# Token groups of 256 and 272, a tail by token groups, down's first operands ahead of up's last pairs, and the residual's squares taken in down

## The chip, the cores and the metric

The kernel runs on one core of a Trainium2 chip. The metric is the device time of one execution in microseconds (us). The core has five engines with an instruction queue each: TensorE (PE in the profile, with PEld for its weight loads), VectorE (DVE), ScalarE (ACT), GpSimd (POOL) and SyncE (SP), which here does nothing but issue DMA transfers. An engine takes its instructions in the order of its queue. SBUF is the working memory, PSUM the memory that matmuls write to, DRAM the memory outside.

## The reference, cut to what matters

One layer of a streaming encoder over 1056 tokens (1024 of a new stream, 32 of a running one), with a model width of 1024 and a feed-forward width of 4096, all in float32:

```python
h = rms_norm(x, ln1_g)
proj = h @ w_in                       # q, k, v of 4 heads; a, b of a gated unit
u = proj_a * sigmoid(proj_b)
a = diff_attention(q, k_all, v_all)   # two softmaxes per head, their difference times v
c = conv(u); c = layer_norm(c); c = c * sigmoid(c)
x = x + concat([a, c]) @ w_out        # output projection
h2 = rms_norm(x, ln2_g)
x = x + square(relu(h2 @ w_up)) @ w_down
y = rms_norm(x, ln_f_g)               # y, and k, v and the last frames of u, are returned
```

## The kernel before

Activations lie transposed, with channels on the 128 partitions and tokens along the free dimension. Every matrix product is made of three: both operands are split into a high and a low part of a faster float type (`split`, `split_to`, `w_split`: a copy on ScalarE for the high part, a subtraction on VectorE or GpSimd for the low part), and high·high, high·low and low·high are summed in PSUM (`products`, L101, and `mm1`, L987). The work is written in program order; a framework gives each engine's queue its order by a simulation of the whole kernel, so instructions of one engine may stand in another order than written, and it gives tiles their slots: a pool has so many slots (`bufs`), and a new tile waits until a slot's earlier tile was read for the last time.

The stages are these.

*Start.* `x_load` loads token tiles of 128 (the ninth has 32), `x_stat` takes the sum of squares of each token (L262), `x_group` transposes a set of tiles (`XSET`: three, two, two, two tiles), copies it to SBUF (L282) and makes the normalized operand with its split (L291 to L296). `load_block` loads and splits a block of `w_in`.

*Dense.* `dense` multiplies a block of 128 output channels with one of four token groups (`GRP`: four times 264 columns; `GW` is 264 and `HT` 528, half of the tokens). Attention, convolution and their norms run between the blocks. The first two blocks run group by group, as `x_group` delivers.

*Output projection.* Parts of `w_out` are multiplied early (`out_part`, L832); the loop at L956 does the rest by token group and block `ob`, adds into the residual stream `x2` (L962) and calls `rows_in`, which squares the sum on ScalarE (L907), adds the squares up over the blocks on GpSimd into `ssacc` (L908), scales by the norm's weight and splits. `b_sums` (L919) makes sums of the operand's quarters on VectorE, `spill` stores `x2` to DRAM as `x2d`. The row's scale is not applied before up: it is squared by the activation and taken out in the final norm, so down's residual is scaled by it instead.

*Up and down.* Both products go by seven products of half blocks instead of eight. Up's operands are named by these products, 1 to 7 (`BX`), and lie in tiles of 128x4x528 ("quads") in three pools, `act[0]` and `act[1]` with four slots each and `q2` with eight. Up runs over sixteen pairs of 128 output channels. Each pair stores seven tiles of results to DRAM (`ud`); the last two pairs run step by step side by side. `row_stat` (L1107) sums `ssacc` over the partitions, and `row_scales` loads the result back in two forms: `vb`, on all partitions, and `rs2`, a column per final tile (L1189).

Down runs over four chunks (`c`) of seven products each, in the order 1, 2, 6, 7, 4, 5, 3 (`PRODS`). A product has four units `m` of 24 matmuls of 264 columns. Its operand is loaded from `ud` (`u_load`, L1220) and split (`u_split`); its weights are loaded from `w_down` (`d_a`), summed (L1232 to L1235) and split. `d_run` runs a product and adds it to its accumulators (L1244). At four products (`RES`) a quarter of the residual is loaded from `x2d`, scaled by `vb` (L1201) and added (L1204).

*Tail.* `final(j)` is the last norm of one token tile of `FT`: eight transposes (L1297), squares with their sum on ScalarE (L1302), a step on VectorE (L1303), the power −1/2 on GpSimd (L1304), two products on VectorE (L1305, L1306), and the store. In the last chunk `fin_step` puts these between the units: tiles 0 to 4 from product 5 on, 5 to 7 in the second half of product 3, 8 to 10 behind everything.

Of the kernel before, what the change touches and what calls it, by code (L numbers as in the profile page):

```python
# [51 lines left out]
def hybrid_step(ctx: ExitStack, tc: tile.TileContext, t):  # L52
# [72 lines left out]
    def act_groups(hi, lo):  # L125

        return [
            [[a[k // 4][g // 2][:, k % 4, GW * (g % 2) : GW * (g % 2) + GW] for k in range(KC)] for a in (hi, lo)]
            for g in range(4)
        ]  # L130
# [636 lines left out]
    x_load(2)  # L767
# [5 lines left out]
    for j in range(3):  # L773
        x_stat(j)
# [94 lines left out]
    sqp = ph2.enter_context(tc.tile_pool(name="sqp", bufs=2, reuse_waits="tile"))  # L869
    ssacc = bigp.tile([P, TOK], F32, tag="big", name="ssacc")  # L870
# [29 lines left out]
    def rows_in(ob, c0, n):  # L900

        xs = x2[ob][:, c0 : c0 + n]
        if ob == 0:
            nc.scalar.activation(ssacc[:, c0 : c0 + n], xs, AF.Square)
        else:
            sq = sqp.tile([P, GW], F32, tag="sq", name="sq2")[:, 0:n]
            nc.scalar.activation(sq, xs, AF.Square)  # L907
            nc.gpsimd.tensor_tensor(ssacc[:, c0 : c0 + n], ssacc[:, c0 : c0 + n], sq, ALU.add)  # L908
        kh, k, th, s = ob // 4, ob % 4, c0 // HT, slice(c0 % HT, c0 % HT + n)
        nc.scalar.activation(B[kh][th][:, k, s], xs, AF.Copy, scale=pcol[:, 12 + ob : 13 + ob])  # L910
        if th == 0:
            split_to(B[kh][0][:, k, s], Bs[kh][0][:, k, s], Bs[kh][1][:, k, s])
# [42 lines left out]
    for g in range(4):  # L955
        for ob in range(3, KC):  # L956
            ps = psM.tile([P, 512], F32, tag="mm", name="pw")
            v = ps[:, 0:GW]
            products(v, wo[ob], PARTS[2] if ob < 6 else [4, 5, 6, 7, 0, 1, 2, 3], slice(0, P), *cx[g])
            c0, w = GRP[g]  # L960
# [22 lines left out]
    def mm1(out, w, b, hb, first):  # L983

        seq = [(w[i], b[j], k) for i, j in ((0, 0), (0, 1), (1, 0)) for k in range(4)]
        for n, (wi, bj, k) in enumerate(seq):
            nc.tensor.matmul(  # L987
                out, wi[:, k, :], bj[:, k, GW * hb : GW * hb + GW],
                start=first and n == 0, stop=n == len(seq) - 1, skip_group_check=not first,
            )  # L990

    def mm(ps, w, b, first):

        for hb in range(2):
            mm1(ps[:, hb, 0:GW], w, b, hb, first)
# [63 lines left out]
    def up_steps(p, ws, ps1):  # L1059
# [25 lines left out]
        t3 = tTp.tile([P, HT], F32, tag="tT", name="o3")  # L1085
        sub(p1, pre, u11)
        sub(t3[:], c22, p1)
        store(p, 0, t0)
        dma(ud[6, p], t3[:])
# [5 lines left out]
        sub(pre, c21, t3[:])  # L1095
        store(p, 4, t2)

    rsd = dram.tile([1, TOK], F32, tag="rsd", name="rsd")

    def row_stat():  # L1100

        v = bigp.tile([P, 2, HT], F32, tag="big", name="vrow")
        for th in range(2):
            ps = acc_tile()
            for hb in range(2):
                c0 = HT * th + GW * hb
                nc.tensor.matmul(ps[0:1, hb, 0:GW], ones[:], ssacc[:, c0 : c0 + GW], start=True, stop=True)  # L1107
            nc.vector.tensor_scalar(halves(v[0:1, th, :]), ps[0:1, :, 0:GW], 1.0 / D, EPS, ALU.mult, ALU.add)
        dma(rsd[:], v[0:1].rearrange("p b n -> p (b n)"))
# [28 lines left out]
    up_load(1, act[0])  # L1138
    nxt = up_s(0, False)
    up_p2(*pend1)  # L1140
    row_stat()

    for p in range(NP_ - 2):
        ws = nxt
        ps1 = up_p1(p) if p >= NPRE else None
        up_load(p + 2, (q2, act[0])[p % 2])
        if p + 1 < NP_ - 2:
            nxt = up_s(p + 1, p + 1 >= NPRE)
        for _ in up_steps(p, ws, ps1):
            pass  # L1150
    last = [NP_ - 2, NP_ - 1]
    by = {}
# [28 lines left out]
    FT = [(P * j, P) for j in range(4)] + [(4 * P, HT - 4 * P)] + [(HT + 88 * j, 88) for j in range(6)]  # L1181
    rs2 = sm2.tile([P, 16], F32, tag="rs2", name="rs2", bufs=1)
    vb = lnp.tile([P, TOK], F32, tag="vb", name="vb")

# [30 lines left out]
    UVAR = {1: 0, 2: 4, 6: 6, 7: 2, 4: 5, 5: 1, 3: 3}  # L1215
    ops_u, raw_u = {}, {}

    def u_load(c, i):
        raw_u[c, i] = quad(act[0], "du")[:]
        dma(raw_u[c, i], ud[UVAR[i], 4 * c : 4 * c + 4].rearrange("k p n -> p k n"))  # L1220

    def u_split(c, i):
        ops_u[c, i] = split_to(raw_u.pop((c, i)), quad(q2, "dh", F32R)[:], quad(q2, "dl", F32R)[:])

# [28 lines left out]
    held = {}  # L1253

    def d_run(c, i, w):
        end = c == NCH - 1
        u = ops_u.pop((c, i))
        if end and i == 3:

            for hb in range(2):  # L1260
                for m in range(4):
                    if m % 2 == 0:
                        ps = acc_tile()
                    mm1(ps[:, m % 2, 0:GW], w[m], u, hb, True)
                    add(ACC[5][m][:, GW * hb : GW * hb + GW], ps[:, m % 2, 0:GW])
                    fin_step()
                if hb == 0:
                    fin.extend([lambda: None] + [lambda j=j: final(j) for j in range(5, 8)])
            return
        second = i in (2, 4, 3)  # L1270
        for m in range(4):
            ps = held.pop(m) if second else acc_tile()
            if i in (1, 7, 5) and not (end and i == 5):
# [8 lines left out]
            if end and i == 5:  # L1282
                add(halves(ACC[5][m]), v)
                fin_step()
# [3 lines left out]
        if end and i == 4:  # L1288
            fin.extend([lambda: None] + [lambda j=j: final(j) for j in range(5)])


    def final(j):
# [7 lines left out]
        ss = sm2.tile([P, 2], F32, tag="ssf", name="ssf")[:n, 0:1]  # L1300
# [14 lines left out]
    for c in range(NCH):  # L1315

        loads.extend([
            [("a", c, 0), ("u", c, 1)], [("a", c, 1), ("u", c, 2)], [("a", c, 2), ("a", c, 3), ("u", c, 6)],
# [8 lines left out]
    RES = {(1, 2): (0, 0), (1, 4): (1, 0), (2, 2): (0, 1), (2, 4): (1, 1)}  # L1327
    load_step()
    load_step()
    u_split(*seq[0])  # L1330
    nw = w_prep(*seq[0])
    for n, (c, i) in enumerate(seq):
# [5 lines left out]
        if (c, i) == (0, 3):  # L1338
            row_scales()
# [5 lines left out]
        d_run(c, i, w)  # L1345
        if (c, i) in RES:
# [3 lines left out]
    for j in range(8, 11):  # L1350
        final(j)
# [65 lines left out]
```

## Time and profile before

| | |
|---|---|
| time, median of 3 runs | 1224.98 us (1224.97 to 1226.77) |
| profiled execution: its own time | 1224.9 us |
| its span, from the first to the last instruction | 1223.1 us |
| mean granted clock of TensorE | 0.994 of full speed |
| TensorE busy | 1176.2 us, 96% of the span, 9340 matmuls |
| VectorE busy | 887.9 us, 73% |
| ScalarE busy | 580.9 us, 47% |
| GpSimd busy | 142.1 us, 12% |
| DMA | 157.15 MB, 128 GB/s in the mean |

The profile is of one execution on the chip. Busy time counts an engine's instructions, without its waits. Matmuls are pipelined and the profile's ends are modelled, so the duration of one (about 0.28 us) is longer than the distance from one start to the next. A releaser in the lists of waits is inferred from semaphores.

### The profile page before, as it was taken

To read this page: it belongs to the slowest core of one execution; us is meant where nothing else is said; L and a number is where in the kernel's file an instruction comes from. 1 tells how busy PE (TensorE), PEld (TensorE's weight loads), DVE (VectorE), ACT (ScalarE), POOL (GpSimd) and SP (SyncE) were. 2 spreads that over 40 slices of the span, in tenths; PEclk is the share of its full clock that TensorE was granted. 3 is DMA by queue.
4 is the path that set the end of the run, shared out by engine and by line. 5 is a ranking of instruction groups with operands and counts; after the bars stand their busy time and mean duration, and the time that the engine had idled before them with its cause. 6 is when DMAs were issued, how large, how long until landed. Compare 5 with 4: busy or idle time off the path is not lost. (4 is left out here: it accounts for less than half of the span.)

```text
span 1223.1 us, 23089 instructions
## 1 busy us (share of the span) xinstructions
PE 1176.2 (96%) x9340; PEld 1131.1 (92%) x9340; DVE 887.9 (73%) x1494; ACT 580.9 (47%) x1160; POOL 142.1 (12%) x149
## 2 busy tenths in 40 slices
PE   6999999999899999989999999999999999999995
PEld 5889988898888789989999999999999999999995
DVE  5797795799975644687776565665865978978865
ACT  7434345433488543665444444444745343333323
POOL 3111122022231221350000000000000000000001
PEclk9999999999999999999999999999999999999998
DMA  6531122122233422234554343445964354454003
GB/s 221 194 101 53 37 66 80 54 62 60 64 110 111 125 89 69 107 97 139 197 190 156 135 152 140 149 142 184 330 225 150 135 188 171 160 193 141 18 23 120
DMA packets 126410, 157.15 MB, mean 128 GB/s; under 512 B 7889, under 2 KB 79458, under 8 KB 126304
## 3 DMA queue, kind: packets, MB, share of 16 engines
q1 hardware_dynamic: 124640, 152.74, 37.3%
q0 software_dynamic: 1664, 2.95, 0.9%
q8 instruction: 73, 1.20, 0.4%
q14 instruction: 33, 0.27, 0.1%
HBM read 104.32 MB, written 51.35 MB: 127 GB/s over the span
## 5 line engine op out<-in xcount | busy, mean ns | idle before, releaser
L987 PE MATMUL pf<-dh,wlo 128*128 128x264 f32 x896 | 144.9, 284 | 2.8 <-DVE wlo L877 2.8
L987 PE MATMUL pf<-dl,whi 128*128 128x264 f32 x896 | 146.9, 286 | 0.0
L987 PE MATMUL pf<-dh,whi 128*128 128x264 f32 x896 | 146.3, 286 | 0.0
L876 ACT ACTIVATE whi<-da 128x512 fp32r<-128x512 f32 x96 | 60.3, 631 | 145.2 <-PE pf L987 141.0
L987 PEld LDWEIGHTS pf<-dh,wlo 128*128 128x128 f32 x896 | 124.1, 189 | 3.0 <-DVE wlo L877 3.0
L987 PEld LDWEIGHTS pf<-dl,whi 128*128 128x128 f32 x896 | 125.0, 189 | 0.0
L987 PEld LDWEIGHTS pf<-dh,whi 128*128 128x128 f32 x896 | 123.4, 189 | 0.1
L101 PE MATMUL pm<-hTh,whi 128*128 128x264 f32 x640 | 107.3, 294 | 6.9 <-ACT tT L347 2.3
L876 ACT ACTIVATE whi<-praw 128x512 fp32r<-128x512 f32 x86 | 53.6, 628 | 107.8 <-PE pf L987 61.6
L78 POOL TENSOR_TENSOR wlo<-raw,whi 128x512 fp32r<-128x512 f32 (+1 forms) x55 | 77.4, 1422 | 229.0 <-PE pm L101 161.0
L101 PE MATMUL pm<-hTh,wlo 128*128 128x264 f32 x640 | 103.8, 287 | 0.0
L101 PE MATMUL pm<-hTl,whi 128*128 128x264 f32 x640 | 102.2, 286 | 1.0 <-DVE hTl L296 1.0
L101 PEld LDWEIGHTS pm<-hTh,whi 128*128 128x128 f32 x640 | 87.2, 188 | 14.0 <-issue 3.2
L101 PEld LDWEIGHTS pm<-hTl,whi 128*128 128x128 f32 x640 | 87.3, 188 | 2.1 <-DVE hTl L296 1.4
L101 PEld LDWEIGHTS pm<-hTh,wlo 128*128 128x128 f32 x640 | 87.8, 188 | 1.3 <-issue 1.3
L1067 DVE TENSOR_TENSOR o<-pf,o 128x528 f32<-128x528 f32 x80 | 56.1, 703 | 44.9 <-PE pf L987 44.7
L1304 POOL TENSOR_TENSOR ssf<-ssf,mhalf 88x1 f32<-88x1 f32 (+2 forms) x11 | 6.0, 547 | 669.4 <-DVE ssf L1303 669.4
L877 DVE TENSOR_TENSOR wlo<-praw,whi 128x512 fp32r<-128x512 f32 x86 | 58.6, 685 | 27.4 <-ACT whi L876 13.4
L877 DVE TENSOR_TENSOR dl<-du,dh 128x2112 fp32r<-128x2112 f32 x28 | 65.9, 2354 | 9.8 <-ACT dh L876 9.4
L1244 DVE TENSOR_TENSOR xa<-pf,xa 128x528 f32<-128x528 f32 (+1 forms) x72 | 48.0, 671 | 34.0 <-PE pf L987 33.9
L877 DVE TENSOR_TENSOR wlo<-da,whi 128x512 fp32r<-128x512 f32 x96 | 64.9, 681 | 10.5 <-ACT whi L876 5.5
L531 ACT ACTIVATE p<-ps,mn 128x128 f32<-128x128 f32 (+6 forms) x64 | 47.4, 742 | 35.2 <-DVE mn L524 30.8
(300 smaller groups left out, 2732.8 us busy)
## 6 DMA issues: line engine op xcount, KB each, us to landing
du<-ud SPq DMA_DIRECT2D x28, 1056.0 KB, 6.0
ud<-o SPq DMA_DIRECT2D x48, 528.0 KB, 3.9
praw<-in_w_up SPq DMA_DIRECT2D x16, 1024.0 KB, 5.5
da<-in_w_down SPq DMA_DIRECT2D x16, 1024.0 KB, 7.5
raw<-in_w_in SPq DMA_DIRECT2D x40, 256.0 KB, 3.0
xTd<-xT SPq DMA_DIRECT2D x8, 528.0 KB, 2.7
x<-xTd SPq DMA_DIRECT2D x8, 528.0 KB
x2d<-x SPq DMA_DIRECT2D x16, 264.0 KB, 2.0
```

The lines of the kernel that those rows point to most:

```text
L78: (eng or nc.vector).tensor_tensor(lo[:], raw, hi[:].bitcast(F32), ALU.subtract)
L101: nc.tensor.matmul(out, w[k][a][:, cols], b[k], start=i == 0, stop=i == len(seq) - 1)
L531: nc.scalar.activation(p[:, 0:nk], sc[m], AF.Exp, bias=mn[:, 2 + m : 3 + m], scale=-1.0, accum_out=s0 if m == 0 else s1[:, 0:1],)
L876: nc.scalar.activation(hi, raw, AF.Copy)
L877: nc.vector.tensor_tensor(lo, raw, hi.bitcast(F32), ALU.subtract)
L987: nc.tensor.matmul(out, wi[:, k, :], bj[:, k, GW * hb : GW * hb + GW], start=first and n == 0, stop=n == len(seq) - 1, skip_group_check=no ...
L1067: add = lambda o, ps, b: nc.vector.tensor_tensor(halves(o), ps, halves(b), ALU.add)
L1244: nc.vector.tensor_tensor(o, ps, o, ALU.add)
L1304: nc.gpsimd.tensor_tensor(ss, ss, mhalf[:n, 0:1], ALU.pow)
```

## The change

- `GRP` becomes (0, 256), (256, 272), (528, 272), (800, 256), and `XSET` two, three, two, two tiles. The third token tile is loaded with the second set. The sums of squares of tiles 0 and 1 are taken on VectorE.
- The squares and their sums in `rows_in` are left out. In down, at the products in `SQR`, a quarter of `x2d` is loaded, squared on ScalarE and summed on VectorE into `vb`; `row_stat` and `row_scales` come after product 6 of the second chunk, and the residual steps at later products.
- Two quads of up lie in other pools. Ahead of the last two pairs, down's operands (0, 1) and (0, 2) are loaded into `q2`, and the first is split there. The last pairs' tile `o3` lies in `q2` too.
- The last chunk's products 5 and 3 run over tokens in two groups (`LAST`: 272 and 256 columns), both products of a group together; product 3 is summed onto product 5 in PSUM. `FT` has ten tiles, of which two stand behind the last matmul. The statistic of `final` has five slots instead of two.

```diff
-GRP = tuple((GW * g, GW) for g in range(4))
+GRP = ((0, 256), (256, 272), (528, 272), (800, 256))
-XSET = ((0, 1, 2), (3, 4), (5, 6), (7, 8))
+XSET = ((0, 1), (2, 3, 4), (5, 6), (7, 8))
@@ x_stat(j)
-        nc.scalar.activation(ac[:n, j % 4, 0:D], xts[j][:n], AF.Square, accum_out=ss[:n])
+        if j < 2:
+            nc.vector.tensor_tensor_reduce(
+                ac[:n, j % 4, 0:D], xts[j][:n], xts[j][:n], 1.0, 0.0, ALU.mult, ALU.add, ss[:n]
+            )
+        else:
+            nc.scalar.activation(ac[:n, j % 4, 0:D], xts[j][:n], AF.Square, accum_out=ss[:n])
@@ start
     x_load(1)
-    x_load(2)
-    for j in range(3):
+    for j in XSET[0]:
         x_stat(j)
@@ rows_in(ob, c0, n)
-        if ob == 0:
-            nc.scalar.activation(ssacc[:, c0 : c0 + n], xs, AF.Square)
-        else:
-            sq = sqp.tile([P, GW], F32, tag="sq", name="sq2")[:, 0:n]
-            nc.scalar.activation(sq, xs, AF.Square)
-            nc.gpsimd.tensor_tensor(ssacc[:, c0 : c0 + n], ssacc[:, c0 : c0 + n], sq, ALU.add)
@@ b_sums, to_x, up_load: pools
-                T[i] = quad(act[0], f"T{i}")
+                T[i] = quad(act[i // 4], f"T{i}")
-            6: (T[2], act[1], act[1]), 7: (B[0][1], act[1], act[1]), 5: (T[1], act[0], q2), 4: (T[4], q2, act[0]),
+            6: (T[2], act[1], act[1]), 7: (B[0][1], act[1], act[0]), 5: (T[1], act[0], q2), 4: (T[4], q2, act[0]),
-        up_load(p + 2, (q2, act[0])[p % 2])
+        up_load(p + 2, (q2, act[1])[p % 2])
@@ up_steps
-        t3 = tTp.tile([P, HT], F32, tag="tT", name="o3")
+        t3 = o3q[:, 2 * (p % 2), :] if p >= NP_ - 2 else tTp.tile([P, HT], F32, tag="tT", name="o3")[:]
@@ up, ahead of the last two pairs
-    row_stat()
...
     last = [NP_ - 2, NP_ - 1]
+    o3q = quad(q2, "o3q")
+    u_load(0, 1, q2)
+    u_split(0, 1)
+    u_load(0, 2, q2)
@@ down
-    FT = [(P * j, P) for j in range(4)] + [(4 * P, HT - 4 * P)] + [(HT + 88 * j, 88) for j in range(6)]
+    FT = [(P * j, P) for j in range(4)] + [(4 * P, HT - 4 * P)]
+    FT += [(HT, 91), (HT + 91, 91), (HT + 182, 90), (HT + 272, P), (HT + 400, P)]
+    def squares(kh, th):
+        x = xq.pop((kh, th))
+        v = vb[:, HT * th : HT * th + HT]
+        nc.scalar.activation(x[:], x[:], AF.Square)
+        nc.vector.tensor_tensor(x[:, 0:2, :], x[:, 0:2, :], x[:, 2:4, :], ALU.add)
+        if kh:
+            nc.vector.tensor_tensor(v, v, x[:, 0, :], ALU.add)
+            nc.vector.tensor_tensor(v, v, x[:, 1, :], ALU.add)
+        else:
+            nc.vector.tensor_tensor(v, x[:, 0, :], x[:, 1, :], ALU.add)
+    LAST = ((0, 272, (5, 6, 7)), (272, 256, (8, 9)))
@@ d_run(c, i, w), last chunk
+        if end and i == 5:
+            last5[:] = w, u
+            return
         if end and i == 3:
-            for hb in range(2):
-                for m in range(4):
-                    if m % 2 == 0:
-                        ps = acc_tile()
-                    mm1(ps[:, m % 2, 0:GW], w[m], u, hb, True)
-                    add(ACC[5][m][:, GW * hb : GW * hb + GW], ps[:, m % 2, 0:GW])
-                    fin_step()
-                if hb == 0:
-                    fin.extend([lambda: None] + [lambda j=j: final(j) for j in range(5, 8)])
+            for c0, n, tiles in LAST:
+                for a, wu in ((4, last5), (5, (w, u))):
+                    for m in range(4):
+                        if a == 4 and m % 2 == 0:
+                            held[m] = held[m + 1] = acc_tile()
+                        ps = held[m][:, m % 2, 0:n]
+                        mm1(ps, wu[0][m], wu[1], c0, n, a == 4)
+                        add(ACC[a][m][:, c0 : c0 + n], ps)
+                        fin_step()
+                fin.extend([lambda j=j: final(j) for j in tiles])
             return
@@ final(j)
-        ss = sm2.tile([P, 2], F32, tag="ssf", name="ssf")[:n, 0:1]
+        ss = sm2.tile([P, 1], F32, tag="ssf", name="ssf", bufs=5)[:n]
@@ the loop of down
-    RES = {(1, 2): (0, 0), (1, 4): (1, 0), (2, 2): (0, 1), (2, 4): (1, 1)}
+    SQR = {(0, 6): (0, 0), (0, 4): (1, 0), (0, 3): (0, 1), (1, 2): (1, 1)}
+    STAT = 1, 6
+    RES = {(1, 5): (0, 0), (2, 2): (1, 0), (2, 4): (0, 1), (2, 3): (1, 1)}
-        if (c, i) == (0, 3):
-            row_scales()
+        if (c, i) in SQR:
+            residual_load(*SQR[c, i])
         d_run(c, i, w)
+        if (c, i) in SQR:
+            squares(*SQR[c, i])
+        if (c, i) == STAT:
+            row_stat()
+            row_scales()
```

## Rows read from the trace of the kernel before

**Rows 1.** Busy time by stretch: length, PE, PEld, DVE, ACT, POOL (instructions), clock, DMA, GB/s.
```profile
15.40:28.00 12.60, 10.69 (x76) 9.27 (x76) 11.73 (x29) 12.60 (x35) 5.25 (x8) 1.00 0.61 207
306.80:309.45 2.65, 0.34 (x2) 0.14 (x2) 2.65 (x8) 1.11 (x5) 0.00 (x0) 1.00 0.46 137
529.60:533.20 3.60, 3.60 (x17) 3.60 (x18) 3.60 (x4) 2.61 (x6) 3.44 (x4) 0.53 0.40 152
825.00:850.00 25.00, 25.00 (x206) 25.00 (x205) 13.85 (x22) 12.21 (x21) 0.00 (x0) 1.00 0.43 160
888.82:891.92 3.10, 0.29 (x3) 0.07 (x1) 3.10 (x4) 0.00 (x0) 0.00 (x0) 0.94 0.64 232
891.92:895.00 3.08, 3.08 (x14) 3.08 (x15) 2.97 (x5) 1.11 (x2) 0.00 (x0) 0.50 0.82 241
895.00:920.00 25.00, 25.00 (x208) 25.00 (x207) 13.22 (x15) 11.90 (x16) 0.00 (x0) 1.00 0.68 239
1030.00:1110.00 80.00, 80.00 (x662) 80.00 (x661) 68.02 (x77) 30.43 (x35) 0.00 (x0) 1.00 0.50 175
```

**Rows 2.** Timeline of the start: begin, duration, engine, line, operation [idle before, releaser].
```profile
8.89 1.06 ACT L262 ACTIVATE ac<-xt 128x1024 f32<-128x1024 f32 x1 [3.39 <-DMA xt<-in_x_prompt]
15.38 0.51 PE L101 MATMUL pm<-hTh,whi 128*128 128x264 f32 x2 [0.34 <-ACT hTh L295]
```

**Rows 3.** TensorE's waits over the span: who waited for whom, total, times, longest (us).
```profile
PE pw L101 <- DVE x L962: 3.1, 1, 3.1
PE pf L987 <- DVE wlo L877: 2.8, 1, 2.8
```

**Rows 4.** Timeline of the tail, from 1204 on.
```profile
1204.42 0.43 DVE L1244 TENSOR_TENSOR xa<-pf,xa 128x264 f32<-128x264 f32 x1 [1.03 <-PE pf L987]
1206.17 0.65 PE L987 MATMUL pf<-dh,wlo 128*128 128x264 f32 x4
1208.23 1.95 PE L1297 MATMUL pfin<-cst,xa 128*88 128x128 f32 x16 [0.53 <-DVE y L1306]
1215.47 1.28 DVE L1306 SCALAR_TENSOR_TENSOR y<-pfin,ssf,lnfb 88x1024 f32<-88x1024 f32 x1
1217.72 1.28 DVE L1306 SCALAR_TENSOR_TENSOR y<-pfin,ssf,lnfb 88x1024 f32<-88x1024 f32 x1
1219.40 0.36 SPq L1311 DMA_DIRECT2D o_y_sample<-y  x1
```

**Rows 5.** Timeline of TensorE at attention scores of 512 and 256 columns.
```profile
117.62 0.39 PE L515 MATMUL ps<-kql,kqh 64*128 64x512 f32 x2
118.08 0.28 PE L515 MATMUL ps<-kqh 64*128 64x256 f32 x2
118.20 0.28 PE L515 MATMUL ps<-kql,kqh 64*128 64x256 f32 x2
```

**Rows 6.** Output projection: the squares' additions (ns, min/median/max), and two sums in the timeline.
```profile
L908 POOL TENSOR_TENSOR ssacc<-ssacc,sq x28: 750/761/2037, 497.2 to 541.3; 128x264 f32<-128x264 f32 x28
...
518.02 1.25 DVE L919 TENSOR_TENSOR T<-B,B 128x1056 f32<-128x1056 f32 x1
527.42 1.79 DVE L919 TENSOR_TENSOR B<-B,B 128x1056 f32<-128x1056 f32 x1
```

**Rows 7.** Timeline of VectorE from up to down.
```profile
857.48 2.36 DVE L877 TENSOR_TENSOR dl<-du,dh 128x2112 fp32r<-128x2112 f32 x1 [1.38 <-ACT dh L876]
888.91 2.35 DVE L877 TENSOR_TENSOR dl<-du,dh 128x2112 fp32r<-128x2112 f32 x1
```

**Rows 8.** Loads: a kind of issue (count, KB, us to landing), and the timeline.
```profile
du<-ud SPq DMA_DIRECT2D x28, 1056.0 KB, 6.0
...
574.41 7.36 SPq L1189 DMA_DIRECT2D rs<-rsd  x10
983.50 0.36 SPq L1220 DMA_DIRECT2D du<-ud  x1
990.78 1.96 ACT L876 ACTIVATE dh<-du 128x2112 fp32r<-128x2112 f32 x1
```

More of the change, by code (lines that the diff above doesn't have):

```diff
@@ L127, in act_groups @@
         return [
-            [[a[k // 4][g // 2][:, k % 4, GW * (g % 2) : GW * (g % 2) + GW] for k in range(KC)] for a in (hi, lo)]
-            for g in range(4)
+            [[a[k // 4][c0 // HT][:, k % 4, c0 % HT : c0 % HT + n] for k in range(KC)] for a in (hi, lo)]
+            for c0, n in GRP
         ]
@@ L981, in acc_tile, with mm1 @@
         return psF.tile([P, 2, 512], F32, tag="f", name="pf")
-    def mm1(out, w, b, hb, first):
+    def mm1(out, w, b, c0, n, first):
         seq = [(w[i], b[j], k) for i, j in ((0, 0), (0, 1), (1, 0)) for k in range(4)]
-        for n, (wi, bj, k) in enumerate(seq):
+        for i, (wi, bj, k) in enumerate(seq):
             nc.tensor.matmul(
-                out, wi[:, k, :], bj[:, k, GW * hb : GW * hb + GW],
-                start=first and n == 0, stop=n == len(seq) - 1, skip_group_check=not first,
+                out, wi[:, k, :], bj[:, k, c0 : c0 + n],
+                start=first and i == 0, stop=i == len(seq) - 1, skip_group_check=not first,
             )
@@ L994, in mm @@
         for hb in range(2):
-            mm1(ps[:, hb, 0:GW], w, b, hb, first)
+            mm1(ps[:, hb, 0:GW], w, b, GW * hb, GW, first)
         return ps[:, :, 0:GW]
@@ L1094, in up_steps @@
         relu2(c21, c21)
-        sub(pre, c21, t3[:])
+        sub(pre, c21, t3)
         store(p, 4, t2)
[L1098 to L1103, printed above, removed]
-            ps = acc_tile()
-            for hb in range(2):
[L1106 to L1109, printed above, removed]
     def to_x(n):
         raw, ph, pl = {
-            6: (T[2], act[1], act[1]), 7: (B[0][1], act[1], act[1]), 5: (T[1], act[0], q2), 4: (T[4], q2, act[0]),
+            6: (T[2], act[1], act[1]), 7: (B[0][1], act[1], act[0]), 5: (T[1], act[0], q2), 4: (T[4], q2, act[0]),
             3: (B[1][1], act[0], q2),
@@ L1137, in hybrid_step @@
     up_load(0, q2)
-    up_load(1, act[0])
+    up_load(1, act[1])
     nxt = up_s(0, False)
     up_p2(*pend1)
-    row_stat()
     for p in range(NP_ - 2):
@@ L1150, in hybrid_step, with u_load, u_split @@
             pass
+    UVAR = {1: 0, 2: 4, 6: 6, 7: 2, 4: 5, 5: 1, 3: 3}
+    ops_u, raw_u = {}, {}
+    def u_load(c, i, pool=act[0]):
+        raw_u[c, i] = quad(pool, "du")[:]
+        dma(raw_u[c, i], ud[UVAR[i], 4 * c : 4 * c + 4].rearrange("k p n -> p k n"))
+    def u_split(c, i):
+        ops_u[c, i] = split_to(raw_u.pop((c, i)), quad(q2, "dh", F32R)[:], quad(q2, "dl", F32R)[:])
     last = [NP_ - 2, NP_ - 1]
+    o3q = quad(q2, "o3q")
+    u_load(0, 1, q2)
+    u_split(0, 1)
+    u_load(0, 2, q2)
     by = {}
@@ L1179, in hybrid_step, with row_stat @@
         ACC[nm] = [xa[4 * kh + m][:, th, :] for m in range(4)]
-    FT = [(P * j, P) for j in range(4)] + [(4 * P, HT - 4 * P)] + [(HT + 88 * j, 88) for j in range(6)]
-    rs2 = sm2.tile([P, 16], F32, tag="rs2", name="rs2", bufs=1)
+    FT = [(P * j, P) for j in range(4)] + [(4 * P, HT - 4 * P)]
+    FT += [(HT, 91), (HT + 91, 91), (HT + 182, 90), (HT + 272, P), (HT + 400, P)]
+    rs2 = sm2.tile([P, len(FT)], F32, tag="rs2", name="rs2", bufs=1)
     vb = lnp.tile([P, TOK], F32, tag="vb", name="vb")
+    rsd = dram.tile([1, TOK], F32, tag="rsd", name="rsd")
+    def squares(kh, th):
[8 more added lines that the diff above has]
+            nc.vector.tensor_tensor(v, x[:, 0, :], x[:, 1, :], ALU.add)
+    def row_stat():
+        for th in range(2):
+            ps = acc_tile()
+            for hb in range(2):
+                c0 = HT * th + GW * hb
+                nc.tensor.matmul(ps[0:1, hb, 0:GW], ones[:], vb[:, c0 : c0 + GW], start=True, stop=True)
+            v = vb[0:1, HT * th : HT * th + HT]
+            nc.vector.tensor_scalar(halves(v), ps[0:1, :, 0:GW], 1.0 / D, EPS, ALU.mult, ALU.add)
+        dma(rsd[:], vb[0:1, :])
     def row_scales():
@@ L1214, in hybrid_step @@
     PRODS = (1, 2, 6, 7, 4, 5, 3)
[L1215 to L1223, printed above, removed]
     def w_of(c, i):
@@ L1272, in d_run @@
             ps = held.pop(m) if second else acc_tile()
-            if i in (1, 7, 5) and not (end and i == 5):
+            if i in (1, 7, 5):
                 held[m] = ps
@@ L1281, in d_run @@
                 nc.scalar.activation(halves(ACC[a][m]), v, AF.Copy)
-            if end and i == 5:
-                add(halves(ACC[5][m]), v)
-                fin_step()
             if end and i in (6, 7, 4):
@@ L1288, in d_run @@
         if end and i == 4:
-            fin.extend([lambda: None] + [lambda j=j: final(j) for j in range(5)])
+            fin.extend([lambda j=j: final(j) for j in range(5)])
     def final(j):
@@ L1349, in hybrid_step @@
         fin_step()
-    for j in range(8, 11):
-        final(j)
     phd.close()
```

16 lines of the change are left out of this document (6 added, 10 removed).

## The prediction

> **What bounds the kernel now.** I read the busy time by stretch first, then the start, TensorE's waits, and the end. In the middle of the last matrix product TensorE starts 208 matmuls of 264 columns in 25.00 us, 120 ns each, without idle time [rows 1]. There only fewer columns could help, and the change keeps their number. What can move is where TensorE stands still or runs at half clock: the start, before its first dense matmul at 15.38 us [rows 2]; the end of the output projection, where it waits 3.1 us for VectorE's addition at L962; the passage from up to down, where it waits 2.8 us for VectorE's split at L877 [rows 3]; and the last 12 us, a chain of final norms [rows 4]. The reader is to see in [rows 1] that behind both waits the granted clock is at its lower level, 1.2 GHz, for a while (0.53 and 0.50 in the mean of these stretches), and that after the gap of 2.65 us at 306.80 it still is 1.00.
>
> All terms are set against the profiled execution's own 1224.9 us (span 1223.1, and 1.8 around it). The median shown is 1224.98, so the sum stands for it as well.
>
> **Dense groups of 256 and 272.** The four groups still sum to 1056 columns, in as many matmuls. At 264 columns one start follows the other by 120 ns. Score matmuls of 512 columns start about 0.23 us apart and of 256 columns 0.12 (117.62, 118.08, 118.20, two side by side on half the rows each) [rows 5]: half the columns, half the time, so no floor shows at the width used here. If one lay at 120 ns all the same, 256 columns would take 120 and 272 3.3 ns more (8 columns at 2.4 GHz): half of some 2,690 matmuls, 4.5 us lost. A gain has no reason, since the columns are the same. I take 0, by the rows.
>
> **The start.** The first set has two token tiles instead of three: the third tile's 512 KB no longer travel beside the second's, and the squares of tiles 0 and 1 go from ScalarE to VectorE. Before, ScalarE squares tile 1 from 8.89 on (1.06 us, and tile 2 next) ahead of the first weight split [rows 2], and from 15.4 to 28 it is busy 12.60 of 12.60 us [rows 1]: it paces the first two groups. One square of 1.06 leaves its path, and its stream starts about 1 us sooner: 2.0 us. A reduction over 1024 elements on VectorE has no row; the nearest are its product over 1024, 1.28 us [rows 4], and the square itself, 1.06; either fits into VectorE's idle time before the first copies. Against it: the second set now has three tiles, the third lands last, and TensorE may wait between the sets. Ends: 3.5 gained (the square, and the third tile's whole transfer) and 1.0 lost, another square late. I take 2.0 gained.
>
> **Output projection without squares.** 32 squares leave ScalarE and 28 additions (0.76 us in the median, up to 2.04) leave GpSimd [rows 6]. The wait is for an eviction behind two column sums on VectorE; such a sum takes 1.25 us alone (518.02) and 1.79 beside GpSimd's additions (527.42) [rows 6]. Two of them give back 1.1 us, and a wait of 2.0 stays, less than the gap of 2.65 after which the clock stayed up. The lowered clock took 3.60 us from 529.60 on for 17 matmuls [rows 1], which are 2.04 at 120 ns: 1.55 more. Sum 2.65, of which I take 2.5. Ends: 0, if the sums stay ahead and the clock falls all the same, and 4.6, if the eviction goes first and wait and low clock both vanish.
> The Trainium skill (SBUF — State Buffer, "Who interferes with whom") says that a VectorE instruction with two SBUF inputs and a GpSimd one that reads SBUF exclude each other, and the later waits for the other's end. The rows show less than a whole addition lost, 0.54 of 0.76 us per sum; by the rule's full wait the term would be 3.1.
>
> **Up to down.** TensorE stops at 888.82 [rows 1]. The split it waits for, of weights, stands on VectorE behind the third operand's split (888.91, 2.35 us) [rows 7]. The change loads down's first operand ahead of the last two pairs and splits it there; before, that split is the 2.36 us at 857.48 [rows 7]. It goes to before 850, where VectorE is busy 13.85 us of 25 [rows 1], and ScalarE's half of it too. All that follows comes 2.36 us sooner, so 2.82 − 2.36 = 0.5 us of wait is left, and the clock has no reason to fall: from 891.92 on 14 matmuls took 3.08 us [rows 1] instead of 1.68, 1.4 more. Gain 2.4 + 1.4 = 3.8. It rests on slots and queues. The loads and splits use q2, whose eight slots hold up's operands; the first pair of these is read for the last time by the last pairs' first products, so two come free early, for the output quad and the load. On SP the loads stand ahead of the last pairs' stores, on ScalarE the copy ahead of their weight splits: a load that lands late holds these. Ends: 4.2 gained (wait and clock) and 2 lost; late next would be the third operand's split.
>
> **Down: squares, residual, row sums.** Four loads of 1 MB and four squares of 128x2112 on ScalarE are added, 1.96 us each by the copy of that size at 990.78 [rows 8]. On VectorE come four sums of 1.25 [rows 6] and six of half that size, 0.7 each (an estimate from 1.25 and from 2.36 at twice the elements): 9.2 us. VectorE has 12 of 80 us free there [rows 1]; of the four residual steps one more moves into the third chunk, 2.36 + 4 × 0.7 = 5.2 us. That hides, at 0; without this cover it would be all 9.2. The row sums with their broadcast now lie in down. Their ten small loads held SP's queue for 7.36 us; behind them now stands an operand's load, which before was issued at 983.50, 7.3 us ahead of ScalarE's copy at 990.78 [rows 8]. The copy is made about one product (96 × 0.12 = 11.5 us) ahead of its use, which covers most of it. Ends: 0 and 6 lost; I take 1.0 lost.
> The Trainium skill (DMA: Bandwidth & Descriptors, Specifications) puts pieces under 512 B below line rate, and these loads write 4 B pieces. No row here times their transfer. By that rule the loads behind them land later still, which speaks for the last rival.
>
> **The tail.** The last dense matmuls end at 1206.8; the last product on VectorE starts at 1217.72 and takes 1.28 us, to 1219.0, 12.2 us later. One norm there takes 2.25 us (1215.47 to 1217.72) [rows 4]: its statistic has two slots, so every second one waits for the product. Now two tiles stand behind the last matmul instead of four, with five slots. Behind it come: eviction 0.43 [rows 4] and hand-over 0.2 (an estimate), transposes 0.4 (0.12 each) [rows 4], square and readout 1.3 [rows 2], power and the steps around it 2.25 − 1.28 = 1.0, product 1.3, the second tile 1.3 to 2.3: 6.0 to 7.0. I take 7.0. Some 16 transposes more run ahead of the last matmul, 1.9 us, and the last store, 128 rows instead of 88, takes 0.3 more, an estimate from the 3.7 us between 1219.40 [rows 4] and the span's end. Gain 12.2 − 7.0 − 1.9 − 0.3 = 3.0. Ends: 1.0 (the weights of the two last products need sixteen tiles and there are fourteen slots, so one unit comes late) and 4.5.
>
> **Sum.** 2.0 + 2.5 + 3.8 − 1.0 + 3.0 = 10.3; 1224.9 − 10.3 = 1214.6.
>
> **The rivals.** *The stops stay.* q2's slots come too late and the first operand is split where it was, or the sums stay ahead of the eviction and the clock falls at both places. For it: each stop is an order on one queue, and the change doesn't name what stands first there. Against: 2.36 us less stand ahead of the split. Then start, tail and 1.0 us of shorter sums are left: 2.0 + 3.0 + 1.0 − 1.0 = 5.0, so 1220. In this case moving the first operands doesn't do what it says.
> *All goes.* Each gain is at its upper end and SP costs nothing: 3.5 + 4.6 + 4.2 + 4.5 = 16.8, so 1208. For it: ScalarE and GpSimd lose all 60 instructions around the first stop. Against: all four have to be there.
> *Slower: down waits for its loads.* The new loads take slots of act[0], four in all, which the operands and sums need, and stand ahead of the operands' loads. Such a load lands 6.0 us after its issue, and an operand's had 7.3 us to its copy [rows 8]: 1.3 to spare. From the point where the copy's lead of a product is used up, TensorE stops for 6.0 − 1.3 = 4.7 us at each new load, and the clock adds 1.4: 6.1 each, with four 24.4, so 1239; two make 1227. Against: the kernel before makes four such loads for the residual, and TensorE is busy 80.00 of 80 us beside them [rows 1].
>
> **Chances.** Forecast 0.56 (1210 to 1219), stops stay 0.20 (1217 to 1224), all goes 0.15 (1205 to 1210), waits for loads 0.09 (1225 to 1239). A measurement of this kernel tells about 0.2%, 2.5 us, from no change. Faster: 0.56 + 0.15 + 0.14 of the stops = 0.85. Same: 0.05 of the stops and 0.01 of the loads = 0.06. Slower: 0.01 + 0.08 = 0.09. The range 1206 to 1222 leaves out the loads' 0.09 and about 0.1 at the ends of the others.
>
> **What would show it.** Right: no half clock in the middle of the span; no wait of TensorE over 1 us for VectorE near 526 and 889; a first dense matmul near 13; two norms behind the last dense matmul, and at most 7 us to the last product's end. Wrong: a new wait of TensorE for a split whose operand was loaded late, in down's first three chunks; a gap between the first two dense groups; a mean pace above 120 ns in the groups of 256 and 272.

## The result and the profile after

The changed kernel takes 1216.67 us (median of 4 runs, 1214.84 to 1217.96) against 1224.97; ratio 0.9918, 95% interval 0.9891 to 0.9944. The forecast was 1214.6, with 1206 to 1222 as its range. The profiled execution after took 1217.96, its span is 1216.2 (before 1223.1).

Two traces are best compared by counting TensorE's matmuls of each stage, from 0, and reading when the same one starts. Differences to the trace of before in us, minus is earlier; the second column is a second profile of the same kernel (below), the third the changed kernel with the old start and groups:

```
matmul                      before     after   again   old start, 264
first dense                  15.38     -1.52   -0.61   -0.93
240th dense                  59.81     -0.70   +0.02   -0.94
last dense                  400.21     +4.25   +1.94   -0.82
first of output projection  499.59     +3.58   +0.39   -2.14
400th of up                 589.83     -3.20   -6.42   -8.93
96th of down                881.09     -3.17   -6.39   -8.90
192nd of down               897.27     -7.57  -10.78  -13.30
1344th of down             1037.13     -4.44   -7.65  -10.17
2496th of down             1176.97     -4.44   -7.65  -10.17
span's end                 1223.13     -6.94  -10.15  -12.67
```

From the first of the output projection on, the changed kernel moves by the same steps in all three columns: 6.8 gained up to up's 400th matmul, 4.4 between down's 96th and 192nd, 3.1 lost in down, 2.5 gained at the end. The dense stage differs from one execution to the next, and there the change lost.

TensorE's waits after, which answer to [rows 3] (who waited for whom; total, times, longest in us):

```profile
PE ps L521 <- DVE kql L366: 3.9, 3, 1.6
PE pm L102 <- ACT tT L353: 2.2, 1, 2.2
PE pw L102 <- DVE x L959: 1.7, 1, 1.7
```

The wait for VectorE's addition is 1.7 instead of 3.1, and the one for a weight split in down is gone. What is largest in total now is the split of the attention's keys (kql); it was there before too, with 2.9 in three waits.

Stretches after, which answer to [rows 1] (length; PE, PEld, DVE, ACT, POOL busy with instructions; clock, DMA share, GB/s):

```profile
74.94:78.36 3.42, 3.42 (x18) 3.42 (x17) 3.42 (x5) 0.00 (x0) 0.00 (x0) 0.50 0.02 5
293.40:296.82 3.42, 3.42 (x18) 3.42 (x17) 2.26 (x3) 0.05 (x1) 0.00 (x0) 0.50 0.02 5
334.36:337.78 3.42, 3.23 (x15) 3.24 (x16) 3.11 (x9) 1.38 (x5) 0.69 (x1) 0.50 0.00 0
526.50:536.50 10.00, 8.34 (x69) 8.09 (x68) 6.70 (x11) 3.61 (x7) 0.00 (x0) 1.00 0.34 112
875.00:900.00 25.00, 25.00 (x206) 25.00 (x205) 24.32 (x26) 13.77 (x18) 0.00 (x0) 1.00 0.99 345
```

The last two are the places of the two stops: full clock in both, and no idle time at the second. But three stretches of the dense stage run at 1.2 GHz, half the clock, for 3.42 us each, where the trace of before had full clock up to 529. Half of 3 × 3.42 is 5.1 us, and the stage from the 240th to the last dense matmul is 4.95 longer.

The column sums, the first operand's split and the row sums in the timeline after, for [rows 6 to 8]:

```profile
529.12 1.25 DVE L916 TENSOR_TENSOR T<-B,T 128x1056 f32<-128x1056 f32 x1
530.29 1.25 DVE L916 TENSOR_TENSOR B<-B,B 128x1056 f32<-128x1056 f32 x1
...
842.26 2.36 DVE L880 TENSOR_TENSOR dl<-du,dh 128x2112 fp32r<-128x2112 f32 x1 [1.59 <-PE pf L984]
...
984.08 1.94 PE L1206 MATMUL pf<-vb,ones 128*1 128x264 f32 x8
988.45 5.80 SPq L1215 DMA_DIRECT2D rs<-rsd  x10
```

And the tail, for [rows 4]:

```profile
1204.33 0.63 PE L984 MATMUL pf<-dh,wlo 128*128 128x256 f32 x4
...
1208.15 1.28 DVE L1326 SCALAR_TENSOR_TENSOR y<-pfin,ssf,lnfb 128x1024 f32<-128x1024 f32 x1
1209.35 0.14 DVE L1323 TENSOR_SCALAR ssf<-ssf 128x1 f32<-128x1 f32 x1
1209.58 0.55 POOL L1324 TENSOR_TENSOR ssf<-ssf,mhalf 128x1 f32<-128x1 f32 x1 [1.71 <-DVE ssf L1323]
1210.42 1.28 DVE L1326 SCALAR_TENSOR_TENSOR y<-pfin,ssf,lnfb 128x1024 f32<-128x1024 f32 x1
```

Down's last matmul ends at 1204.96, the last product on VectorE at 1211.70: 6.7 us, where 12.2 were before.

### The profile page after: what moved, and what is told of

Read it like the earlier page. It is cut to its first block, busy times and chain, and to the rows that moved or that the text cites. A ratio compares the mean times of both kernels' runs of the same rounds, so it can differ in the third digit from the quotient of the medians.

```text
span 1216.2 us, 22991 instructions
## 1 busy us (share of the span) xinstructions
PE 1182.7 (97%) x9332; PEld 1134.7 (93%) x9332; DVE 888.0 (73%) x1505; ACT 575.4 (47%) x1126; POOL 119.9 (10%) x120
## 4 chain that ended last, share of the span: by engine, by line
PE 84%; DVE 9%; DMA 1%; issue 1%; ACT 1%; POOL 0%; ACTq 0%; POOLq 0%; DVEq 0%
PE pf L984 54%; PE pm L102 18%; PE ps L521 3%; PE pw L102 3%; DVE ac L440 2%; PE po L558 2%; DVE ac L446 2%; DVE ac L453 2%; PE pat L554 1%; PE pfin L1317 1%; DMA catl<-ascr 1%; PE pss L643 1%; DVE ps L530 0%; PE pln L465 0%; DVE p L544 0%
## 5 line engine op out<-in xcount | busy, mean ns | idle before, releaser
L984 PE MATMUL pf<-dh,whi 128*128 128x264 f32 (+2 forms) x896 | 146.5, 286 | 0.0
L984 PE MATMUL pf<-dl,whi 128*128 128x264 f32 (+2 forms) x896 | 146.3, 285 | 0.0
L984 PE MATMUL pf<-dh,wlo 128*128 128x264 f32 (+2 forms) x896 | 144.9, 283 | 0.0
L102 PE MATMUL pm<-hTh,whi 128*128 128x256 f32 (+1 forms) x640 | 107.5, 295 | 4.5 <-ACT tT L353 2.2
L102 PE MATMUL pm<-hTh,wlo 128*128 128x256 f32 (+1 forms) x640 | 106.6, 292 | 0.0
L102 PE MATMUL pm<-hTl,whi 128*128 128x256 f32 (+1 forms) x640 | 105.6, 291 | 0.0
L79 POOL TENSOR_TENSOR wlo<-raw,whi 128x512 fp32r<-128x512 f32 (+1 forms) x55 | 81.5, 1496 | 235.8 <-PE pm L102 158.9
L102 PEld LDWEIGHTS pm<-hTh,wlo 128*128 128x128 f32 x640 | 90.3, 193 | 1.3 <-issue 1.2
L1324 POOL TENSOR_TENSOR ssf<-ssf,mhalf 128x1 f32<-128x1 f32 (+3 forms) x10 | 5.5, 548 | 714.9 <-DVE ssf L1323 714.9
L1260 DVE TENSOR_TENSOR xa<-pf,xa 128x528 f32<-128x528 f32 (+2 forms) x72 | 46.1, 642 | 32.7 <-PE pf L984 32.1
```

What stands on the lines that cost most here:

```text
L79: (eng or nc.vector).tensor_tensor(lo[:], raw, hi[:].bitcast(F32), ALU.subtract)
L102: nc.tensor.matmul(out, w[k][a][:, cols], b[k], start=i == 0, stop=i == len(seq) - 1)
L984: nc.tensor.matmul(out, wi[:, k, :], bj[:, k, c0 : c0 + n], start=first and i == 0, stop=i == len(seq) - 1, skip_group_check=not first,)
L1260: nc.vector.tensor_tensor(o, ps, o, ALU.add)
```

## Experiments

The disputed points: whether the groups of 256 and 272 cost the 5 us of the dense stage or the half clock fell there by chance, and which part brought what. Medians, runs, and ratio to the kernel before with its interval:

```
old start and groups in the changed kernel   1212.61   4  0.9895  0.9877 to 0.9913
start and groups alone                       1227.23  10  1.0012  0.9999 to 1.0025
squares in down alone                        1222.28  10  0.9976  0.9963 to 0.9989
first operands alone                         1221.10  10  0.9966  0.9953 to 0.9979
tail alone                                   1223.85  10  0.9989  0.9971 to 1.0007
changed kernel again                         1216.10   4  0.9916  0.9889 to 0.9943
keys' split on GpSimd                        1229.01  10  1.0018  1.0005 to 1.0031
old start and groups, GpSimd, shorter tail   1219.43   5  0.9936  0.9915 to 0.9957
old start and groups, shorter tail           1211.63   6  0.9890  0.9870 to 0.9910
  the same, keys' split in two halves        1211.08   6  0.9881  0.9860 to 0.9902
new groups, old start                        1215.56   6  0.9915  0.9895 to 0.9935
five slots in the old tail                   1224.15  10  0.9992  0.9977 to 1.0006
```

**The old start and groups in the changed kernel.**

```diff
-GRP = ((0, 256), (256, 272), (528, 272), (800, 256))
-XSET = ((0, 1), (2, 3, 4), (5, 6), (7, 8))
+GRP = tuple((GW * g, GW) for g in range(4))
+XSET = ((0, 1, 2), (3, 4), (5, 6), (7, 8))
...
```

The lines left out put the third token tile's load and all squares back to where they were.

> The changed kernel with the start and the dense groups of before: four groups of 264, three token tiles in the first set, all squares of the start on ScalarE. All else is changed. In the changed kernel the stage from the first to the last dense matmul is 390.6 us long, against 384.8 before; three stretches at half clock of 3.4 us each (1.7 lost in each) make 5.1 of that. Theory (the short waits for the split of the attention's keys, kql, which both kernels have, make TensorE fall to half clock in some schedules and not in others): the group sizes cost nothing by themselves; the stage is 384.8 plus 1.7 for each stretch at half clock, and the pace between is 120 ns. Rival (the groups of 256 and 272 cost): the stage is 384.8, with no half clock in it. By both the first dense matmul is back at 15.4, so the time is 1216.7 - 4.3 = 1212.4 if no half clock shows, and up to 1217.5 if three do.

It ran 1212.61 and is faster than the changed kernel: this part of the change costs something. One stretch at half clock showed, at 308, behind the wait of 2.64 after which the clock of before had stayed up [rows 1]. So groups of 264 don't keep the clock up by themselves, which speaks for the theory; but the time came out at the rival's.

**Start and groups alone**, the same edit the other way, on the kernel before.

> The kernel before with only the start and the groups changed (groups of 256 and 272, two token tiles in the first set, two squares on VectorE). Theory of the waits: the first dense matmul at 13.85; the stage of the dense products loses 1.7 us per stretch at half clock behind a wait for kql, none to three of them: 1223.5 to 1228.6. Rival, the groups cost: 4.3 us lost at the last dense matmul, 1229. What the start itself gains is read at the 240th dense matmul, before attention begins: 0.7 by the changed kernel's trace, 2.0 by the prediction.

1227.23, 1.6 above before, with the interval just touching no change. Three stretches at half clock in the dense stage again (72.11, 290.57, 311.05; a fourth lay at the start, at 14), and 1.9 lost at its end.

**Squares in down alone.**

```diff
 def rows_in(ob, c0, n):
-    nc.scalar.activation(sq, xs, AF.Square)
-    nc.gpsimd.tensor_tensor(ssacc[...], ssacc[...], sq, ALU.add)
...
+    if (c, i) in SQR:
+        squares(*SQR[c, i])
```

> The kernel before with only the residual's squares, their sums, the row sums and the residual's steps moved to down. Prediction: 2.5 gained at the output projection, 1.0 lost in down: 1223.5. Rival, the gain of 7.4 us that the changed kernel shows between the first matmul of the output projection and the 400th of up comes from this part alone (wait for the eviction 3.1 to 1.7, no half clock there, the wait of 1.2 for ScalarE gone, and 1.9 of the row sums' matmuls that only move): 7.4 gained at up's 400th matmul, 1.9 back in down and 1.2 more lost there, so 1220.6. If down's loads paid for it, SP's ten small loads would show a wait of TensorE for an operand's split in chunks 1 and 2.

1222.28. From the first of the output projection to up's 400th matmul it gains 5.95. Down's first products then wait for ScalarE's copies of the first accumulators and for a weight split:

```profile
PE pf L979 <- ACT xa L1285: 2.9, 3, 2.3
PE pf L979 <- DVE wlo L875: 2.0, 1, 2.0
```

The copies stand in ScalarE's queue behind the first square, and that square waits for its load, which landed 8.8 us after its issue at 873.28:

```profile
882.11 1.97 ACT L1170 ACTIVATE xq<-xq 128x2112 f32<-128x2112 f32 x1 [3.63 <-DMA xq<-x2d]
884.50 0.59 ACT L1285 ACTIVATE xa<-pf 128x528 f32<-128x528 f32 x1
```

The next two squares wait for their loads too (5.79 and 6.50 us of ScalarE). So here a new load did hold down's first products, as the slower rival had it, though for 2.3 us once and not 4.7 at each load. In the changed kernel ScalarE never waited for the squares' loads: the first square starts 7.0 us after its load's issue, without idle time before it. That the early operands do this, by what else stands in the queues, is argued and not tested.

**First operands alone**: pools, `o3q`, and `u_load` and `u_split` ahead of the last pairs.

> The kernel before with only the pools' change and down's first operands loaded and split ahead of up's last pairs. Prediction: no wait over 0.5 us and no half clock at the passage from up to down, 3.8 gained: 1221.2. Rival (the slots come too late, or the clock falls all the same): nothing gained, 1225, with the wait of 2.8 still behind the split, or 1.4 gained where only the wait becomes short. Up itself should be as long as before.

1221.10, as predicted: no wait and no half clock at the passage, 4.4 gained there, and up is as long as before. But its trace loses 3.2 again between down's 192nd and 2496th matmul, without a gap (below), and gains 1.2 in the output projection, which the edit doesn't touch; so that the time agrees is in part luck.

**The changed kernel again**, no edit.

> The changed kernel once more, unaltered, for a second profile and for times beside the other kernels of this set. What the first set showed: in four profiles of kernels with groups of 264 the wait of 1.87 us at 72 was followed by half clock in two, the wait of 2.64 at 307 in three, with the waits themselves equal to 0.02 us. Theory (whether the clock falls behind a wait of 1.5 to 2.7 us changes from one execution to the next): the waits stand where they stood, and at least one of the three stretches at half clock of the dense stage comes or goes. Rival (it is fixed by the kernel): the same three, at 75, 293 and 334. Median 1216.7 within 1.

This is what settles the half clock. The waits near 290 and 308 are as long as they were (1.96 and 2.44 from start to start, now 1.97 and 2.43); the one at 72 is 1.59 instead of 1.88, and one of 1.38 at 331 is now under 1. The clock of the same three stretches and of a fourth is:

```profile
74.94:78.36 3.42, 3.42 (x31) 3.25 (x29) 3.42 (x7) 0.57 (x2) 0.00 (x0) 1.00 0.02 6
293.40:296.82 3.42, 3.32 (x27) 2.95 (x27) 3.27 (x8) 1.10 (x3) 0.00 (x0) 1.00 0.02 5
311.30:314.72 3.42, 3.42 (x17) 3.42 (x17) 3.42 (x8) 1.06 (x3) 0.00 (x0) 0.50 0.00 0
334.36:337.78 3.42, 3.42 (x30) 3.24 (x30) 3.19 (x12) 3.14 (x9) 0.85 (x1) 1.00 0.00 0
```

Three gone, one come. At 290 and 308 the wait before was the same, so there it doesn't decide the clock by its length. Nor does the chip: the four runs of this set, on one chip, had mean granted clocks of 0.991 to 0.996. In eleven profiles whose order at these places is comparable, sorted by the distance from one matmul's start to the next across the wait:

```
groups of 264 (7 profiles):         1.87-1.88 at 72: half clock in 5; 1.48-1.50 at 290: 0; 2.64 at 307: 5
groups of 256 and 272 (4 profiles): 1.59-1.95 at 72: half clock in 3; 1.96-1.97 at 290: 2; 2.40-2.44 at 307: 3
```

The seven are before, each part alone without the groups (three), five slots, and the two with the old start and groups; the four are the two of the changed kernel, the groups with either start. Dense stages of 264 columns have 14 half clocks in seven profiles, 2.0 each, of 256 and 272 nine in four, 2.25; four of the 14 and one of the nine lie elsewhere, between 332 and 394. The profile of before, with none, was a lucky one.

**Keys' split on GpSimd**, to take the waits for kql away.

```diff
-nc.vector.tensor_tensor(lo[:, 0:NT], src[:, 0:NT], hi[:, 0:NT].bitcast(F32), ALU.subtract)
+for c0 in (0, 512):
+    c = slice(c0, c0 + 512)
+    nc.gpsimd.tensor_tensor(lo[:, c], src[:, c], hi[:, c].bitcast(F32), ALU.subtract)
```

> The changed kernel with the keys' split (kql, 128x1024, 1.22 us on VectorE behind the convolution) moved to GpSimd, in two halves. Theory of the waits: the waits for kql (3.9 us in three) go, and with them the half clock at 75 and 293 (1.7 each): 2 to 3.9 for the waits and up to 3.4 for the clock, as far as TensorE had nothing to do then; 1211.5 to 1214.5. Rival (GpSimd takes longer than VectorE, queues behind its own weight splits and slows VectorE beside it): the waits stay or grow, 1217 or more. Rival, the group sizes cost at every matmul: the waits go and no more than 3 us come back.

1229.01, a miss. The waits for kql fell from 3.9 to 0.9, but a longer one came, since the whole stage's order changed with it and the queries' split on VectorE (L343, which writes a kql too) now stands behind steps of the convolution:

```profile
PE pm L102 <- DVE kql L343: 7.0, 2, 4.1
```

The test says nothing on what the clock does when only the wait goes.

**Tail alone**: `LAST`, ten final tiles, five slots.

> The kernel before with only the tail changed: the last two products by token groups of 272 and 256, ten final tiles, five statistic slots. Prediction: 3.0 gained, 1222.0. Read in the changed kernel's trace: 7.0 us from the last matmul's end to the last product's end instead of 12.2, and 2.6 lost ahead of it (more transposes, and the unit that waits), 2.5 in all: 1222.5. Rival (the units of the two last products come late for want of slots): TensorE waits over 1 us for a weight split in the last 25 us, and the gain falls under 1.

1223.85, interval open to no change. The trace shows the gain all the same: 2.2 from down's 2496th matmul to the span's end, against 2.5 in the changed kernel. No TensorE wait over 1 us for a weight split in the last 25 us.

**Five slots in the old tail.**

```diff
-ss = sm2.tile([P, 2], F32, tag="ssf", name="ssf")[:n, 0:1]
+ss = sm2.tile([P, 1], F32, tag="ssf", name="ssf", bufs=5)[:n]
```

> The kernel before with five slots for the statistic of the final norms instead of two, nothing else. The tail's step of the prediction (every second statistic waits for a slot that the product before it holds) is put to the test: with five, the last norms on VectorE come 1.6 apart (product, and the two short steps) instead of 2.25, so with four products behind the last matmul 1.3 to 2.0 us go: 1223.5. Rival (the order on VectorE sets the distance, not the slot): 2.25 stays between the last products, under 0.5 gained.

1224.15, not told from no change by time, but in the timeline of VectorE the products stand 1.44 apart, not 2.25 [rows 4]:

```profile
1217.35 1.28 DVE L1306 SCALAR_TENSOR_TENSOR y<-pfin,ssf,lnfb 88x1024 f32<-88x1024 f32 x1
1218.56 0.15 DVE L1305 TENSOR_TENSOR ssf<-ssf,rs 88x1 f32<-88x1 f32 x1
1218.79 1.28 DVE L1306 SCALAR_TENSOR_TENSOR y<-pfin,ssf,lnfb 88x1024 f32<-88x1024 f32 x1
```

From the last dense matmul's start to the span's end it is 15.4 us instead of 16.6. The slot did hold the norms apart.

**New groups, old start**, to tell the two apart.

> The changed kernel with groups of 256 and 272, but the old start: three token tiles in the first set, and all squares on ScalarE. It tells the start from the groups. If the groups make the loss: about 1.1 us later than the changed kernel, which is what the new start gains up to the 240th dense matmul in the mean of the profiles so far, so 1217.5; 4 to 5 above the version with groups of 264. If the new start makes it (the third tile late, or the two squares on VectorE): near 1212.6.

1215.56 (ratio 0.9915). It stands by the changed kernel (0.9918 and 0.9916) and not by the one with groups of 264 (0.9895): the loss is the groups', and the new start gave nothing that the times tell. The intervals overlap, so the size is only bounded: 1.6 by the groups and start alone, 4 by the medians of the reverse test, 2.8 by its ratio, which is the safer figure since those medians are of two sets of runs.

**Old start and groups, GpSimd, shorter tail.**

> A version made from the findings: the changed kernel with the start and the groups of 264 of before, the keys' split on GpSimd, and in the last final tile the step after the sum of squares on ScalarE instead of VectorE, so that it doesn't stand behind the product of the tile before. Against 1212.6 of the kernel with the old start: 1.5 to 3 for the waits for kql and their clock, 0.7 in the tail: 1208.5 to 1210.5. If the keys' split on GpSimd is late, 1212 or more; the tail then shows its part by itself, in the time from the last matmul to the last product's end, 6.3 us instead of 7.0.

1219.43, a miss as on GpSimd above: the waits for the keys' split fell to 0.9 and others came, the longest, 2.5, for ScalarE (`ACT p`, L534). The tail did its part, 10.7 from the last dense matmul's start to the end instead of 11.5.

**Old start and groups, shorter tail.** In the last tile the step after the sum of squares goes to ScalarE:

```diff
+if j == len(FT) - 1:
+    nc.scalar.activation(ss, ss, AF.Copy, scale=1.0 / D, bias=EPS)
+else:
     nc.vector.tensor_scalar(ss, ss, 1.0 / D, EPS, ALU.mult, ALU.add)
```

> The changed kernel with the start and the groups of 264 of before, and in the last final tile the step after the sum of squares on ScalarE instead of VectorE. The order of TensorE's work is that of the kernel with the old start (1212.6) up to the last tiles. Expected: 0.8 us less from the last matmul's end to the span's end, 10.7 instead of 11.5, so 1211.8. Rival, the run before it gained its 0.8 in the tail by another schedule: 11.5 again, 1212.6.

1211.63. The last two products now stand 1.46 apart, and the tail is 10.7:

```profile
1202.36 1.28 DVE L1325 SCALAR_TENSOR_TENSOR y<-pfin,ssf,lnfb 128x1024 f32<-128x1024 f32 x1
1203.56 0.15 DVE L1324 TENSOR_TENSOR ssf<-ssf,rs 128x1 f32<-128x1 f32 x1
1203.82 1.28 DVE L1325 SCALAR_TENSOR_TENSOR y<-pfin,ssf,lnfb 128x1024 f32<-128x1024 f32 x1
```

**The same with the keys' split in two halves** on VectorE.

> As the version with the old start and the shorter tail, but the keys' split on VectorE in two halves of 512 columns, 0.6 us each, of which the first scores need one. Theory: the waits of 1.87 and 1.50 for it become 0.6 shorter each, and the half clock behind the first, seen in three of five profiles with groups of 264, shows in fewer; 1.2 for the waits and 0.5 to 1.7 for the clock, 1209.5. Rival (each new instruction reorders the queues of the dense stage, and other waits come): the sum of TensorE's gaps over 1 us between 60 and 405 is as long as before or longer, 1212 or more.

1211.08, not told from the one above. The first wait became 1.34 and was not followed by half clock, the second went; 1.12 and 1.48 came elsewhere (89, 328), one at 168 grew to 1.60, and the idle time in gaps over 1 us from 60 to 405 is 10.2 instead of 9.3. Two half clocks showed as in the version above, at 331 and 393 instead of 73 and 309. All runs of both versions are faster than all eight of the changed kernel; the medians differ by 4.5 to 5.6, the ratios by 3.2 to 4.5 us.

## Why the prediction was right, and where it was not

The total was only 2 us off by luck: errors cancelled. Term by term (gain predicted, gain measured in the trace after):

- **Dense groups, 0: 4.95 lost in this trace, 1.9 in the second, 1.6 to 4 by the times of the two reverse tests.** The step's reason held: the pace is 117.7 ns at 256 columns and 125.5 at 272, 121.6 in the mean, and 121.8 at 264. There is no floor. What failed is that the pace was the whole cost: the edit shifts the queues, and the wait near 290 grew from 1.50 to 1.97, one that never lowered the clock in seven profiles to one that did in two of four; that is half a stretch of 1.7 more there, though over the whole stage the counts differ by only 0.25, 0.4 us. With 1.7 taken off for every half clock, the stage is still 1.3 longer (339.9 against 338.6 in the means; 339.3 to 340.6 in four profiles, 337.8 to 340.4 in seven). Where these 1.3 are stays open.
- **The start, 2.0: 0.** The row at 8.89 [rows 2] was one draw of a load. The moment at which TensorE goes on with the first token tiles lies between 6.3 and 9.2 in the ten profiles with the old start and between 6.4 and 8.2 in the four with the new one; from there to the first dense matmul it takes 6.4 to 6.9 us with either. ScalarE's square was not what the first matmul waited for.
- **Output projection, 2.5: 6.8, of which 2.1 only moved.** The wait fell by 1.4 (3.37 to 1.94 from start to start) and the half clock of 1.7 went; none showed there in the nine profiles without the squares, and one in each of the five with them. The sums take 1.25 both, as foreseen; by that the lengthening was GpSimd's additions, in line with the Trainium skill (SBUF — State Buffer, "Who interferes with whom"), which has such a sum and a GpSimd instruction that reads SBUF exclude each other. Missed was a third stop, 1.5 from start to start at 544.71 before, for a copy on ScalarE behind squares: 1.4 more against this trace. It too differs between the five profiles with squares there: 1.5 in two, 0.6 in two, none over 0.5 in one. And the row sums' eight matmuls at 0.22 each, with the wait behind them 2.1, left this place for down: the prediction moved the row sums but priced only their loads.
- **Up to down, 3.8: 4.4.** The mechanism as stated; the operand is split at 842, none of the 0.5 us of wait that the prediction left is there, and the upper end (4.2) was passed by 0.2.
- **Down, 1.0 lost: 3.1 lost.** SP's ten loads (5.80 us) cost TensorE nothing. 2.1 are the row sums' matmuls. The other 1.0 is pace, without one gap: 122.3 ns per matmul instead of 121.4 from the 192nd to the 1344th. In the mean, down's matmuls start either 121.4 or 122.8 ns apart. From about 830 on it is 122.8 in every profile; in the kernel before it becomes 121.4 behind the half clock at 892, in the changed kernel only behind the row sums at 985, and with the first operands alone it stays 122.8 to down's end. In 80 us that is 662 matmuls [rows 1] or 654, here of the changed kernel, the first operands alone, and five slots:

```profile
900.00:980.00 80.00, 80.00 (x654) 80.00 (x653) 58.69 (x62) 41.32 (x49) 0.00 (x0) 1.00 0.54 193
1030.00:1110.00 80.00, 80.00 (x654) 80.00 (x653) 67.74 (x78) 30.11 (x34) 0.00 (x0) 1.00 0.48 168
1030.00:1110.00 80.00, 80.00 (x654) 80.00 (x653) 67.40 (x76) 28.69 (x34) 0.00 (x0) 1.00 0.50 171
```

The last of these has no early operands. Its stop at the passage is there (2.81), but no half clock followed it, and the slower pace went on as well. So the early operands aren't the cause by themselves: the pace stayed slow in the profiles without the half clock at the passage, and was 121.4 behind it in the three that had it. A part of what this trace gains at the passage is thus lost again in down; what sets the pace is open.
- **Tail, 3.0: 2.5.** 12.2 to 6.7 behind the last matmul (7.0 predicted), 2.6 lost ahead of it (1.9 predicted), 0.4 at the store. The slots mattered, by the test, though in the new tail the two last norms still stood 2.27 apart, by VectorE's order.

Of the rivals, "the stops stay" and "waits for loads" are out for the changed kernel; the second showed once in the squares alone. "All goes" was nearer for the two stops; the start, down, the tail and the groups fell short of it.

Of the prediction's own signs two didn't come: half clock did show in the middle of the span, three times in the dense stage, and the first dense matmul came at 13.86 and, in the second profile, 14.77. The sign "a mean pace above 120 ns" was set too low to tell anything, since groups of 264 have 121.8.

## What to carry to other kernels

Take a wait's half clock as a chance per execution, read from several profiles, and not as a property of one trace: a profile with none may only be lucky. Price moved work by every instruction it issues on every engine, the small matmuls too, and look for all stops of a queue when a load leaves it, not only the longest. Before a start is credited with time, anchor both traces at the landing of the first load.

## What the runs showed of the hardware

The granted clock behind the same wait differed between executions of one program, in stretches of 3.42 us, with TensorE busy in all of them. Waits of 1.9 us (264 columns) were followed by it at one place (72) in 5 of 7 profiles and at another (the output projection, 1.95) in 0 of 9. The wait at the passage from up to down, 3.09 from start to start, was followed by it before and not with five slots. Matmuls of 264 columns in an unbroken stream started 121.4 ns apart in some stretches and 122.8 in others, at full clock in both. A matmul of 264 columns on plain f32 operands starts 0.22 us after the one before, against 0.12 for the split ones.
